# Smaller buffers for the modulation sums and the latents' weights, and the rotary tables on VectorE beside the second output gates

## The chip, the cores and the metric

The kernel runs on one core of one Trainium2 chip. The metric is the device time of one execution in microseconds (us), as a median over several executions. The engines that appear below are PE (TensorE: matrix products and transposes), DVE (VectorE), ACT (ScalarE), POOL (GpSimd) and SP (SyncE, which here only issues transfers between device memory and the core's on-chip buffers).

## The reference, cut to what matters

A trunk of two layers over 1,024 tokens of width 1,024, everything in f32. Layer 0 is an mLSTM mixer and an MLP, layer 1 is latent attention and an MLP, and between them a shared latent key and value is made. Every norm is modulated by sums over a vector `c`, and the rotary tables are a sine and a cosine of position times frequency.

```python
# layer 0: mLSTM mixer
proj = h @ w_in                                # q, k, v, input and forget gates, output gate og
lf = log_sigmoid(f_pre); b = cumsum(lf)        # per chunk of 128 tokens
hh = rmsnorm(mlstm_chunkwise(q, k, v, i_pre, f_pre), head_g)
out = (hh * sigmoid(og)) @ w_out
# every modulated norm: shift, scale and gate come from c
mod = silu(c) @ ada_w + ada_b                  # likewise kv_ada_w for the shared latent
h = rmsnorm(x, g) * (1 + scale) + shift
# shared latent key and value, rotary part
ckv, k_rope = split(h @ w_a); ang = positions[..., None] * inv
k_rope = apply_rope(k_rope, cos(ang), sin(ang))
```

## The kernel before

**Products.** The tokens are handled in two halves of 512 (`hfs[0]`, `hfs[1]`). Every f32 product is three fp32r matmuls (`mm3`, L280 to L282): high part times high part, high times low, low times high. A block of 128 outputs over the width of 1,024 is thus 24 matmuls. A weight block is loaded by SP into a `raw` buffer (128x1024), then `wsplit` copies its high part on ACT (L238, into `wh`) and subtracts on DVE to get the low part (L239, into `wl`).

**Buffers.** The rings that matter are `raw` (4 buffers of 128x1024), `ws` for split weights (8), `tmc` (6 of 128x512), `tma` (1 of 128x512), `hd` (8) and `k` (24, from `k4`), and the PSUM rings `ps`, `pc` and `pm` with 2 each. A buffer is reused when its last reader is done; a load into it waits on SP's in-order queue until then, and everything behind it in that queue waits too.

**Order.** Each engine executes its own instructions in program order. That order is set at build time by a scheduler with priorities (`prompt` raises one); `paced()` says that an instruction of the background may be issued only after a given one of the main work.

**Stages, in time.** The first gates are `gates_in(hfs[0])` and, in it, `gates0`: the 16 gate columns are transposed (L640), and a chain of small DVE and ACT instructions on 8 rows (L694 to L730) ends in transposes on PE (L743). Some POOL memsets clear or fill parts of its tiles (L615, L618, L625, L730). Behind it come values and intra-chunk work (`v_in`; `intra0`, whose exponentials are L769). Before all that, `drain(rope_tables())` has put the whole making of the rotary tables into the program: a position row is turned into angles and reduced by seven steps of a product and a sum of 128x1024 on POOL (L2535, L2536), then two `Sin` on ACT (L2541, L2542). The second output gates are `og0(hfs[1], k4v)`: eight blocks of projection, each followed by Exp, Ln and Exp on ACT (L682 to L684), while `split_o(hfs[1])` multiplies the heads by the gates (L797) and splits them into high (L800) and low part (L801) for the output projection, and `p0` does the first half's residual and norm.

**Background.** `ada_chunk` makes four-times-128 modulation sums: four loads of 128x2x512 of `ada_w` or `kv_ada_w` into `raw` (L377), eight DVE sums into `tma` (L384), then four transposes (L364), a reduction and an addition. `latent_weights` loads six weight blocks of the latent projections into `raw` (L1563), sums them on DVE against the shift (L1567, L1569), scales them on ACT (L1573), splits them with `wsplit` and writes them to device memory from POOL's queue. The steps of both are taken one by one beside the main work:

```python
drain(rope_tables())
drain(with_bg(gates_in(hfs[0]), bgs, 1))
...
for k, _ in enumerate(og0(hfs[1], k4v)):
    if k % 2:
        prompt(next)(so)
    next(bgs)
    if k < 7:
        next(p0)
...
two_streams(f0, behind(bg_latent(), 5))
```

`f0` is the first MLP's sweeps over both halves (about 560 to 880 us). One step of `second` there loads two `raw` buffers of `w1` (L1020) and the first sum (L1025), combines them on DVE (L1026 and on) and makes the weights `wv` by a copy on ACT (L1030) and a subtraction on DVE (L1031); the up projection loads one `raw` buffer per step (L260). What is left of the modulation sums, and `latent_weights`, run beside it.

Of the kernel before, what the change touches and what calls it, by code (L numbers as in the profile page):

```python
# [9 lines left out]
F32 = mybir.dt.float32  # L10
# [4 lines left out]
ALU = mybir.AluOpType  # L15
# [67 lines left out]
def kernel(  # L83
# [286 lines left out]
    late = [False]  # L370

    def ada_chunk(w, c0, bias, dst):

        acc = tma()
        for q in range(4):
            r = raw().rearrange("p (a b) -> p a b", b=512)
            nc.sync.dma_start(r, wcols(w, c0, 512, 2 * q, 2))  # L377
            for kk in range(2):
                k = 2 * q + kk
                with paced():  # L380
                    if k == 0:
                        nc.vector.tensor_scalar(acc, r[:, kk], cond[:, 0:1], None, ALU.mult)
                    else:
                        nc.vector.scalar_tensor_tensor(  # L384
                            acc, r[:, kk], cond[:, k : k + 1], acc, ALU.mult, ALU.add
                        )
            yield
        yield
        late[0] = True
        yield "wait"  # L390
        late[0] = False
        yield from ada_turn(acc, bias, dst)
# [215 lines left out]
    def gates_in(hf):  # L608
# [6 lines left out]
        nc.gpsimd.memset(v7[:, :, 128:VE], 1.0)  # L615
        for t in range(4):
            v = k4()[:, : 7 * VE].rearrange("p (h e) -> p h e", e=VE)
            nc.gpsimd.memset(v[:, :, 128:VE], 1.0)  # L618
            hf.v.append([v[:, h_] for h_ in range(7)] + [v7[:, t], v])
# [5 lines left out]
        nc.gpsimd.memset(g[:, :, :, 8:32], 0.0)  # L625
# [63 lines left out]
    def gates0(hf):  # L689
# [40 lines left out]
        nc.gpsimd.memset(RM.bitcast(F32), 0.0)  # L730
# [822 lines left out]
    def latent_weights():  # L1553
# [4 lines left out]
        for b, vs in enumerate(views):  # L1558
            A, sh = (Akv, kvada[:, 0:8]) if b < 3 else (Aq, adac(1, SH1))
            r_ = raw()  # L1560
            r = r_.rearrange("p (a b) -> p a b", b=P)
            for c0, v in vs:
                nc.sync.dma_start(r[:, :, c0 : c0 + v.shape[2]], v)  # L1563
            yield
            acc = tma()[:, :P]
            with paced():
                nc.vector.tensor_scalar(acc, r[:, 0], sh[:, 0:1], None, ALU.mult)  # L1567
                for k in range(1, KD):
                    nc.vector.scalar_tensor_tensor(  # L1569
                        acc, r[:, k], sh[:, k : k + 1], acc, ALU.mult, ALU.add  # L1570
                    )
            for k in range(KD):
                nc.scalar.activation(r[:, k], r[:, k], AF.Identity, scale=A[:, k : k + 1])  # L1573
            for i, t in enumerate(wsplit(r_, D)):
# [6 lines left out]
            for _ in range(3 if b == 0 else 2):  # L1581
                yield "wait"
# [933 lines left out]
    def rope_tables():  # L2516
# [7 lines left out]
        d, a, kf = hd(), hd(), hd()  # L2524
        pi = d.bitcast(I32)
        nc.gpsimd.tensor_copy(d[:, 0:1], adac(0, SH1)[:, 7:8])
        nc.gpsimd.dma_start(pi, positions.to_broadcast([P, S]))
        nc.gpsimd.tensor_copy(a, pi)
        nc.gpsimd.tensor_scalar(a, a, inv, None, ALU.mult)
        yield  # L2530
        nc.gpsimd.tensor_scalar(kf, a, 1.0 / (2.0 * PI), MAGIC, ALU.mult, ALU.add)
        nc.gpsimd.tensor_scalar_add(kf, kf, -MAGIC)
        for part in TWO_PI_PARTS:
            yield
            nc.gpsimd.tensor_scalar(d, kf, -part, None, ALU.mult)  # L2535
            nc.gpsimd.tensor_add(a, a, d)  # L2536
        yield
        nc.gpsimd.tensor_scalar(a, a, 3.1415925, -3.1415925, ALU.min, ALU.max)
# [6 lines left out]
        nc.gpsimd.tensor_scalar(d, d, sg, None, ALU.mult)  # L2545
# [42 lines left out]
    drain(rope_tables())  # L2588
# [105 lines left out]
    so = split_o(hfs[1])  # L2694
    for k, _ in enumerate(og0(hfs[1], k4v)):
        if k % 2:
            prompt(next)(so)
        next(bgs)
        if k < 7:
            next(p0)  # L2700
# [115 lines left out]
    for v in f0:  # L2816
        if v != "within" and next(p1, end) is end:
            break
    two_streams(f0, behind(bg_latent(), 5))
    rope_perm()  # L2820
# [95 lines left out]
```

## Time and profile before

| | us |
|---|---|
| median of 3 runs | 2339.2 |
| the three runs | 2341.8, 2339.2, 2337.68 |
| the profiled execution | 2336.3 |
| its span, first to last instruction | 2334.1 |

| engine | busy us | instructions |
|---|---|---|
| PE | 2283.2 | 12,042 |
| DVE | 1704.7 | 2,749 |
| ACT | 1126.0 | 1,911 |
| POOL | 146.3 | 231 |

In the views, each instruction has its line, its operation and its tiles as output<-input. A wait is written as the idle time of an engine before an instruction, with the engine and the line that released it; "SPq" is SP's queue, "PEld" PE's weight loads, which overlap its matmuls. Windows give each engine's busy time and instruction count in a stretch, then the granted share of the full TensorE clock, the busy share of the transfer engines and the rate in GB/s.

### The profile page before, as it was taken

What the parts mean: (1) busy time and instruction counts of PE and PEld (TensorE: products, weight loads), DVE (VectorE), ACT (ScalarE), POOL (GpSimd) and SP (SyncE); (2) the same over time, 40 slices, a digit from 0 to 9 for tenths busy, and PEclk for the clock granted to TensorE, in tenths of its full rate; (3) what the DMA queues carried; (4) which work ended last, traced back from release to release, by engine and by line L of the source; (5) the groups of instructions that cost most, each with busy time, mean ns of one, the idle gap of its engine ahead of it and who ended that gap; (6) DMA issues with size and microseconds to landing.
All of it is one profiled execution on the core that took longest, in us unless ns stands there. A gap on an engine that the chain in (4) does not pass through costs nothing.

```text
span 2334.1 us, 32606 instructions
## 1 busy us (share of the span) xinstructions
PE 2283.2 (98%) x12042; PEld 1922.5 (82%) x12042; DVE 1704.7 (73%) x2749; ACT 1126.0 (48%) x1911; POOL 146.3 (6%) x231
## 2 busy tenths in 40 slices
PE   8899999999999999999999999999999999999998
PEld 6788798888877778778888778888888888989997
DVE  6776776879778777678774687765666488798776
ACT  4275334665335355544454464444444444655543
POOL 2700000000112220000000000000000000000000
PEclk9999999999999999999999999999999999999999
DMA  9452464657899888566686754874434452455432
GB/s 328 142 166 82 146 198 139 197 185 230 292 291 296 276 292 301 173 216 213 215 266 188 239 181 149 262 249 136 145 100 136 118 167 81 147 156 166 133 109 109
DMA packets 401103, 444.37 MB, mean 190 GB/s; under 512 B 26579, under 2 KB 288784, under 8 KB 400944
## 3 DMA queue, kind: packets, MB, share of 16 engines
q1 hardware_dynamic: 388000, 397.09, 53.7%
q0 software_dynamic: 12944, 45.20, 5.4%
q8 instruction: 95, 1.56, 0.3%
q14 instruction: 64, 0.52, 0.1%
HBM read 343.65 MB, written 98.57 MB: 189 GB/s over the span
## 4 chain that ended last, share of the span: by engine, by line
PE 77%; DVE 9%; DMA 8%; ACT 2%; issue 2%; SPq 1%; DVEq 0%; ACTq 0%
PE ps L280 13%; PE ps L282 12%; PE ps L281 12%; PE pm L280 9%; PE pm L281 9%; PE pm L282 8%; DMA raw<-in_mlp_w_dram 5%; PE pc L281 2%; PE pc L282 2%; PE pc L280 2%; DVE wl L239 1%; DMA raw<-in_a_w_in_dram 1%; PE pc L1969 1%; DVE k L247 1%; PE pm L1774 1%
## 5 line engine op out<-in xcount | busy, mean ns | idle before, releaser
L239 DVE TENSOR_TENSOR wl<-raw,wh 128x1024 fp32r<-128x1024 f32 (+5 forms) x323 | 382.6, 1187 | 210.2 <-ACT wh L238 185.3
L238 ACT CAST wh<-raw 128x1024 fp32r<-128x1024 f32 (+5 forms) x323 | 327.3, 1017 | 421.0 <-PE ps L281 164.7
L280 PE MATMUL ps<-k,wh 128*128 128x512 f32 (+1 forms) x1252 | 475.7, 380 | 5.6 <-DVE tmp L247 2.8
L282 PE MATMUL ps<-k,wl 128*128 128x512 f32 (+1 forms) x1252 | 467.9, 374 | 0.3 <-DVE wl L239 0.3
L281 PE MATMUL ps<-k,wh 128*128 128x512 f32 (+1 forms) x1252 | 467.7, 374 | 0.1
L280 PEld LDWEIGHTS ps<-k,wh 128*128 128x128 f32 x1252 | 235.9, 188 | 51.6 <-DVE tmp L247 3.6
L282 PEld LDWEIGHTS ps<-k,wl 128*128 128x128 f32 x1252 | 235.8, 188 | 42.9 <-DVE wl L239 0.9
L281 PEld LDWEIGHTS ps<-k,wh 128*128 128x128 f32 x1252 | 236.0, 188 | 41.9 <-issue 1.4
L247 DVE TENSOR_TENSOR k<-k,pm 128x512 f32<-128x512 f32 (+1 forms) x250 | 192.4, 801 | 62.7 <-PE pm L282 62.1
L280 PE MATMUL pm<-wh,hd 128*128 128x512 f32 x488 | 193.4, 396 | 2.6 <-ACT raw L1780 1.5
L282 PE MATMUL pm<-wh,hd 128*128 128x512 f32 x488 | 190.4, 390 | 0.0
L281 PE MATMUL pm<-wl,hd 128*128 128x512 f32 x488 | 190.4, 390 | 0.0
L384 DVE SCALAR_TENSOR_TENSOR tma<-raw,cond,tma 128x512 f32<-128x512 f32 x168 | 126.9, 755 | 23.3 <-DMA raw<-in_ada_w_dram 14.2
L280 PEld LDWEIGHTS pm<-wh,hd 128*128 128x128 f32 x488 | 91.7, 188 | 24.1 <-ACT raw L1780 4.0
L282 PEld LDWEIGHTS pm<-wh,hd 128*128 128x128 f32 x488 | 91.6, 188 | 19.9 <-DVE hd L494 0.5
L281 PEld LDWEIGHTS pm<-wl,hd 128*128 128x128 f32 x488 | 91.8, 188 | 18.4 <-issue 0.5
L281 PE MATMUL pm<-hd,wk 128*128 128x512 f32 x256 | 100.0, 391 | 1.7 <-DVE hd L494 1.7
L280 PE MATMUL pm<-hd,wk 128*128 128x512 f32 x256 | 100.8, 394 | 0.6 <-ACT hd L493 0.6
L1780 ACT ACTIVATE raw<-pm,sm 128x128 f32<-128x128 f32 (+3 forms) x64 | 47.5, 743 | 110.8 <-DVE sm L1779 107.2
L280 PE MATMUL pm<-hd,wh 128*128 128x512 f32 x256 | 99.5, 390 | 0.9 <-DVE tma L384 0.9
L282 PE MATMUL pm<-hd,wl 128*128 128x512 f32 x256 | 99.7, 390 | 0.5 <-DVE wl L239 0.5
L282 PE MATMUL pm<-hd,wk 128*128 128x512 f32 x256 | 99.8, 390 | 0.0
(494 smaller groups left out, 4857.5 us busy)
## 6 DMA issues: line engine op xcount, KB each, us to landing
raw<-in_mlp_w_dram SPq DMA_DIRECT2D x176, 512.0 KB, 4.6
raw<-in_ada_w_dram SPq DMA_DIRECT2D x80, 512.0 KB, 4.8
raw<-in_mlp_w_dram SPq DMA_DIRECT2D x128, 256.0 KB, 4.6
raw<-in_a_w_in_dram SPq DMA_DIRECT2D x44, 512.0 KB, 4.5
lo<-wl POOLq DMA_DIRECT2D x32, 512.0 KB, 7.0
wk<-lo SPq DMA_DIRECT2D x64, 256.0 KB, 3.8
xs<-k SPq DMA_DIRECT2D x40, 256.0 KB, 4.4
raw<-in_a_w_out_dram SPq DMA_DIRECT2D x16, 512.0 KB, 4.5
```

The lines of the kernel that those rows point to most:

```text
L238: nc.scalar.copy(hi[:, :n], r[:, :n])
L239: i = nc.vector.tensor_sub(lo[:, :n], r[:, :n], hi[:, :n].bitcast(F32))
L247: return f(*a, **k)
L280: nc.tensor.matmul(o, lh, rh, start=start, stop=False)
L281: nc.tensor.matmul(o, lh, rl, start=False, stop=False)
L282: pe_last[0] = nc.tensor.matmul(o, ll, rh, start=False, stop=stop)
L384: nc.vector.scalar_tensor_tensor(acc, r[:, kk], cond[:, k : k + 1], acc, ALU.mult, ALU.add)
L1774: nc.tensor.matmul(o[:, :w], qh, kh, start=False, stop=True)
L1780: nc.scalar.activation(pr[:, :n], f, AF.Exp, bias=m, scale=SCALE, accum_out=l)
L1969: nc.tensor.transpose(pt[:, ts(2 * e + i, P)], u.prs[i][:, ts(b + e, P)], ident)
```

## The change

1. The memsets of the gates (L615, L618, L625, L730, of both halves) go from POOL to DVE.
2. `rope_tables` is no longer drained before the first gates. It is stepped twice after each block of the second half's output gates. Its arithmetic goes from POOL to DVE, and each pair of a product and a sum becomes one `scalar_tensor_tensor`. Its tiles come from `k4` in place of `hd`, and a copy that only made it wait is left out. The two `Sin` stay on ACT.
3. `ada_chunk`, while `f0` runs, loads two `tmc` tiles of 128x512 with one transfer each, where it loaded one `raw` buffer.
4. `latent_weights` loads two `tmc` tiles in place of one `raw` buffer, and its scaling and split come one step after its sums; the split is made of halves of 128x512.

```diff
@@ -367,22 +367,28 @@
         nc.vector.tensor_add(dst, s, bias)
         yield
 
-    late = [False]
+    late, apart = [False], [False]
 
     def ada_chunk(w, c0, bias, dst):
 
         acc = tma()
         for q in range(4):
-            r = raw().rearrange("p (a b) -> p a b", b=512)
-            nc.sync.dma_start(r, wcols(w, c0, 512, 2 * q, 2))
+            if apart[0]:
+                r = [tmc(), tmc()]
+                for kk in range(2):
+                    nc.sync.dma_start(r[kk], w[ts(2 * q + kk, P), c0 : c0 + 512])
+            else:
+                r = raw().rearrange("p (a b) -> p a b", b=512)
+                nc.sync.dma_start(r, wcols(w, c0, 512, 2 * q, 2))
+                r = [r[:, 0], r[:, 1]]
             for kk in range(2):
                 k = 2 * q + kk
                 with paced():
                     if k == 0:
-                        nc.vector.tensor_scalar(acc, r[:, kk], cond[:, 0:1], None, ALU.mult)
+                        nc.vector.tensor_scalar(acc, r[kk], cond[:, 0:1], None, ALU.mult)
                     else:
                         nc.vector.scalar_tensor_tensor(
-                            acc, r[:, kk], cond[:, k : k + 1], acc, ALU.mult, ALU.add
+                            acc, r[kk], cond[:, k : k + 1], acc, ALU.mult, ALU.add
                         )
             yield
         yield
@@ -612,17 +618,17 @@
 
         hf.v = []
         v7 = sb.tile([P, 4 * VE], F32, tag="v7", bufs=1, name=f"v7_{hf.i}").rearrange("p (t e) -> p t e", e=VE)
-        nc.gpsimd.memset(v7[:, :, 128:VE], 1.0)
+        nc.vector.memset(v7[:, :, 128:VE], 1.0)
         for t in range(4):
             v = k4()[:, : 7 * VE].rearrange("p (h e) -> p h e", e=VE)
-            nc.gpsimd.memset(v[:, :, 128:VE], 1.0)
+            nc.vector.memset(v[:, :, 128:VE], 1.0)
             hf.v.append([v[:, h_] for h_ in range(7)] + [v7[:, t], v])
         n = 272
         ws_ = [
             wload([(0, 0, wcols(w_in, 1792, n, k0, nk))], n) for k0, nk in ((0, 3), (3, 3), (6, 2))
         ]
         g = tmc()[:, :256].rearrange("p (t a b) -> p t a b", a=2, b=32)
-        nc.gpsimd.memset(g[:, :, :, 8:32], 0.0)
+        nc.vector.memset(g[:, :, :, 8:32], 0.0)
         for t in range(4):
             pt = ps()[:, :n]
             for k in range(KD):
@@ -727,7 +733,7 @@
         nc.vector.tensor_add(enm, b, M)
         nc.scalar.activation(enm, enm, AF.Exp, scale=-1.0)
         RM = hf.RM = tmc(F32R)
-        nc.gpsimd.memset(RM.bitcast(F32), 0.0)
+        nc.vector.memset(RM.bitcast(F32), 0.0)
         nc.vector.tensor_scalar(RM[0:8], M, -1.0, None, ALU.mult)
         nc.vector.scalar_tensor_tensor(
             RM[32:40], M, -1.0, RM[0:8].bitcast(F32), ALU.mult, ALU.subtract
@@ -1557,28 +1563,36 @@
         views += [[(0, wcols(b_w_q_a[0], m * P))] for m in range(3)]
         for b, vs in enumerate(views):
             A, sh = (Akv, kvada[:, 0:8]) if b < 3 else (Aq, adac(1, SH1))
-            r_ = raw()
-            r = r_.rearrange("p (a b) -> p a b", b=P)
+            r = [tmc(), tmc()]
+            cols_ = lambda t: t.rearrange("p (a b) -> p a b", b=P)
             for c0, v in vs:
-                nc.sync.dma_start(r[:, :, c0 : c0 + v.shape[2]], v)
+                for i in range(2):
+                    nc.sync.dma_start(cols_(r[i])[:, :, c0 : c0 + v.shape[2]], v[:, ts(i, 4)])
             yield
             acc = tma()[:, :P]
+            of = lambda k: r[k // 4][:, ts(k % 4, P)]
             with paced():
-                nc.vector.tensor_scalar(acc, r[:, 0], sh[:, 0:1], None, ALU.mult)
+                nc.vector.tensor_scalar(acc, of(0), sh[:, 0:1], None, ALU.mult)
                 for k in range(1, KD):
                     nc.vector.scalar_tensor_tensor(
-                        acc, r[:, k], sh[:, k : k + 1], acc, ALU.mult, ALU.add
+                        acc, of(k), sh[:, k : k + 1], acc, ALU.mult, ALU.add
                     )
+            yield "wait"
+            hi = sb.tile([P, 1024], F32R, tag="ws", bufs=WS, name=f"wh_{next(uid)}")
+            lo = sb.tile([P, 1024], F32R, tag="ws", bufs=WS, name=f"wl_{next(uid)}")
             for k in range(KD):
-                nc.scalar.activation(r[:, k], r[:, k], AF.Identity, scale=A[:, k : k + 1])
-            for i, t in enumerate(wsplit(r_, D)):
+                nc.scalar.activation(of(k), of(k), AF.Identity, scale=A[:, k : k + 1])
+            for i in range(2):
+                nc.scalar.copy(hi[:, ts(i, 512)], r[i])
+                nc.vector.tensor_sub(lo[:, ts(i, 512)], r[i], hi[:, ts(i, 512)].bitcast(F32))
+            for i, t in enumerate((hi, lo)):
                 if b == 2:
 
                     f = lambda t: t.rearrange("p (a b) -> p a b", b=P)[:, :, ts(i, 64)]
                     nc.gpsimd.dma_start(f(lw[b, 0]), f(t).bitcast(F32))
                 else:
                     nc.gpsimd.dma_start(lw[b, i], t.bitcast(F32))
-            for _ in range(3 if b == 0 else 2):
+            for _ in range(2 if b == 0 else 1):
                 yield "wait"
             pt = pc()
             nc.tensor.transpose(pt[:, :P], acc, ident)
@@ -2521,28 +2535,26 @@
         for q in range(4):
             nc.vector.memset(sg[ts(q, 32), :], 1.0 if q % 2 else -1.0)
         MAGIC = 1.5 * 2.0**23
-        d, a, kf = hd(), hd(), hd()
+        d, a, kf = k4()[:,:1024],k4()[:,:1024],k4()[:,:1024]
         pi = d.bitcast(I32)
-        nc.gpsimd.tensor_copy(d[:, 0:1], adac(0, SH1)[:, 7:8])
         nc.gpsimd.dma_start(pi, positions.to_broadcast([P, S]))
-        nc.gpsimd.tensor_copy(a, pi)
-        nc.gpsimd.tensor_scalar(a, a, inv, None, ALU.mult)
+        nc.vector.tensor_copy(a, pi)
+        nc.vector.tensor_scalar(a, a, inv, None, ALU.mult)
         yield
-        nc.gpsimd.tensor_scalar(kf, a, 1.0 / (2.0 * PI), MAGIC, ALU.mult, ALU.add)
-        nc.gpsimd.tensor_scalar_add(kf, kf, -MAGIC)
+        nc.vector.tensor_scalar(kf, a, 1.0 / (2.0 * PI), MAGIC, ALU.mult, ALU.add)
+        nc.vector.tensor_scalar_add(kf, kf, -MAGIC)
         for part in TWO_PI_PARTS:
             yield
-            nc.gpsimd.tensor_scalar(d, kf, -part, None, ALU.mult)
-            nc.gpsimd.tensor_add(a, a, d)
+            nc.vector.scalar_tensor_tensor(a, kf, -part, a, ALU.mult, ALU.add)
         yield
-        nc.gpsimd.tensor_scalar(a, a, 3.1415925, -3.1415925, ALU.min, ALU.max)
+        nc.vector.tensor_scalar(a, a, 3.1415925, -3.1415925, ALU.min, ALU.max)
         nc.vector.scalar_tensor_tensor(kf, a, -1.0, a, ALU.mult, ALU.max)
         nc.vector.tensor_scalar(kf, kf, -1.0, PI / 2, ALU.mult, ALU.add)
         nc.scalar.activation(d, a, AF.Sin)
         last = nc.scalar.activation(kf, kf, AF.Sin)
         with tc.issue_after(last.ins):
             nc.scalar.preload_act_table_set("natural_log_exp_and_others")
-        nc.gpsimd.tensor_scalar(d, d, sg, None, ALU.mult)
+        nc.vector.tensor_scalar(d, d, sg, None, ALU.mult)
         nc.gpsimd.dma_start(rope_d[1], d)
         nc.gpsimd.dma_start(rope_d[0], kf)
         yield
@@ -2585,7 +2597,6 @@
             nc.sync.dma_start(
                 xt_d[0][2 * b * P : (2 * b + 2) * P].rearrange("(k p) n -> p k n", p=P), xT0.t[b]
             )
-    drain(rope_tables())
     drain(with_bg(gates_in(hfs[0]), bgs, 1))
     drain(with_bg(qk_last(hfs[0]), bgs, 1))
     x1 = load_x1()
@@ -2692,10 +2703,13 @@
     ms = [Mlp(0, False)]
     p0 = post(hfs[0], y0, B0, x_ahead(k4v, True), A1, adac(0, SH2), ms[0], (2, 2, 2, 5, 1))
     so = split_o(hfs[1])
+    tables = rope_tables()
     for k, _ in enumerate(og0(hfs[1], k4v)):
         if k % 2:
             prompt(next)(so)
         next(bgs)
+        for _ in range(2):
+            next(tables, None)
         if k < 7:
             next(p0)
     y1 = FH(claim=True)
@@ -2816,7 +2830,9 @@
     for v in f0:
         if v != "within" and next(p1, end) is end:
             break
+    apart[0] = True
     two_streams(f0, behind(bg_latent(), 5))
+    apart[0] = False
     rope_perm()
```

In the order of the program these edits move instructions at three places. Names end in running numbers, which differ between the two kernels.

The first place is POOL at the first gates: `hd_610` to `hd_612` are the table tiles, `k_105` to `k_108` the value tiles. Before:

```order
L2532 TENSOR_SCALAR hd_612<-hd_612 128x1024
L2535 TENSOR_SCALAR hd_610<-hd_612 128x1024
L618 MEMSET k_105_644 128x7x2
L618 MEMSET k_106_646 128x7x2
L618 MEMSET k_107_648 128x7x2
L618 MEMSET k_108_650 128x7x2
L2536 TENSOR_TENSOR hd_611<-hd_611,hd_610 128x1024
L2535 TENSOR_SCALAR hd_610<-hd_612 128x1024
```

Now:

```order
L2533 DMA inv<-in_inv_freq_dram 32x1
L2540 DMA k_656_3940<-in_positions_dram 128x1024
L2558 DMA rope_d<-k_656_3940 128x1024
L2559 DMA rope_d<-k_658_3942 128x1024
L173 MEMSET k_728_4349 128x1
```

POOL has only the transfers of the tables left, and no arithmetic and no memset between the start and the first MLP.

The second place is DVE and ACT at the second output gates, DVE first: `hd_2568` is a head tile that L803 (before: L797) gates, `k_656` to `k_658` are the table tiles. Before:

```order
L797 SCALAR_TENSOR_TENSOR hd_2610<-hd_2610,cols,k_649_3929 128x512
L239 TENSOR_TENSOR wl_4204<-raw_4201,wh_4203 128x1024
L797 SCALAR_TENSOR_TENSOR hd_2610<-hd_2610,cols,k_649_3929 128x512
L801 TENSOR_TENSOR k_668_4015<-hd_2610,k_667_4014 128x1024
L486 TENSOR_SCALAR tmc_4094<-pc_4092 128x512
```

Now:

```order
L803 SCALAR_TENSOR_TENSOR hd_2568<-hd_2568,cols,k_646_3887 128x512
L2541 CAST k_657_3941<-k_656_3940 128x1024
L2542 TENSOR_SCALAR k_657_3941<-k_657_3941,inv 128x1024
L2544 TENSOR_SCALAR k_658_3942<-k_657_3941 128x1024
L2545 TENSOR_SCALAR k_658_3942<-k_658_3942 128x1024
L239 TENSOR_TENSOR wl_4196<-raw_4193,wh_4195 128x1024
L2548 SCALAR_TENSOR_TENSOR k_657_3941<-k_658_3942,k_657_3941 128x1024
L803 SCALAR_TENSOR_TENSOR hd_2568<-hd_2568,cols,k_646_3887 128x512
L2548 SCALAR_TENSOR_TENSOR k_657_3941<-k_658_3942,k_657_3941 128x1024
L807 TENSOR_TENSOR k_668_3991<-hd_2568,k_667_3990 128x1024
```

The table's instructions now stand between the two gatings and the split of one head tile. On ACT, at the last blocks of the same stage, before:

```order
L682 ACTIVATE k_652_3932<-ps_4268 128x512
L683 ACTIVATE k_652_3932<-k_652_3932 128x512
L238 CAST wh_4499<-raw_4497 128x1024
L682 ACTIVATE k_652_3932<-pm_4320 128x512
L684 ACTIVATE k_652_3932<-k_652_3932 128x512
L683 ACTIVATE k_652_3932<-k_652_3932 128x512
L684 ACTIVATE k_652_3932<-k_652_3932 128x512
L800 CAST k_673_4020<-hd_3119 128x1024
```

Now:

```order
L688 ACT_TABLE_LOAD
L688 ACTIVATE k_649_3890<-ps_4260 128x512
L688 ACTIVATE k_649_3890<-pm_4312 128x512
L689 ACT_TABLE_LOAD
L689 ACTIVATE k_649_3890<-k_649_3890 128x512 x2
L690 ACT_TABLE_LOAD
L690 ACTIVATE k_649_3890<-k_649_3890 128x512 x2
L482 ACTIVATE tmc_4248<-hd_3290 128x512
L2554 ACT_TABLE_LOAD
L2554 ACTIVATE k_658_3942<-k_658_3942 128x1024
L2556 ACT_TABLE_LOAD
L806 CAST k_673_3996<-hd_3077 128x1024
```

Five loads of a function table and the second `Sin` (L2554) now stand between the third split of the heads and the last one (L806); the first `Sin` (L2553) with its own load stands ahead of them.

The third place is SP in the first MLP's sweeps, where a step of `second` loads two buffers of `in_mlp_w` and one of `m`. Before:

```order
L1025 DMA k_1066_6224<-m_3924 128x512
L377 DMA raw_6274<-in_ada_w_dram 128x2x512
L377 DMA raw_6278<-in_ada_w_dram 128x2x512
L377 DMA raw_6282<-in_ada_w_dram 128x2x512
L377 DMA raw_6286<-in_ada_w_dram 128x2x512
L1025 DMA k_1089_6329<-m_3924 128x512
L1020 DMA raw_6325<-in_mlp_w_dram 128x8x128
L1020 DMA raw_6326<-in_mlp_w_dram 128x8x128
```

Now:

```order
L1031 DMA k_1081_6217<-m_3882 128x512
L1026 DMA raw_6213<-in_mlp_w_dram 128x8x128
L379 DMA tmc_6318<-in_ada_w_dram 128x512
L379 DMA tmc_6319<-in_ada_w_dram 128x512
L379 DMA tmc_6324<-in_ada_w_dram 128x512
L1026 DMA raw_6214<-in_mlp_w_dram 128x8x128
L379 DMA tmc_6325<-in_ada_w_dram 128x512
L1026 DMA raw_6258<-in_mlp_w_dram 128x8x128
L1031 DMA k_1089_6262<-m_3882 128x512
L1026 DMA raw_6259<-in_mlp_w_dram 128x8x128
L1026 DMA raw_6371<-in_mlp_w_dram 128x8x128
L1026 DMA raw_6372<-in_mlp_w_dram 128x8x128
```

The background's loads no longer take `raw` buffers, and several loads of MLP weights stand in a row behind them. Over the whole of `f0` the background issues 27 loads by L377 and 7 by L1563 before; 54 by L379 and 14 by L1570 now.

## The prediction

> **What bounds the kernel now.** I read the totals first, then PE's waits by stage, then windows and timelines where PE waits.
>
> ```profile
> span 2334.1 us, 32606 instructions
> PE 2283.2 (98%) x12042; PEld 1922.5 (82%) x12042; DVE 1704.7 (73%) x2749; ACT 1126.0 (48%) x1911; POOL 146.3 (6%) x231
> ```
>
> PE is busy 98% of the span, and the change adds and removes no matmul. So only two things can be gained: PE's idle time, 50.9 us in all, and stretches in which the granted clock is low because PE has stood still. What can be lost is any cover that DVE or ACT has now. I therefore ask of each of the three stages that the change touches what PE waits for there.
>
> At the first gates (76 to 150 us), the waits of PE and the windows around them:
>
> ```profile
> PE pc L743 <- DVE tmc L712: 6.1, 1, 6.1
> PE pc L762 <- ACT tmc L769: 1.0, 1, 1.0
> PE pc L743 <- ACT tmc L726: 0.9, 1, 0.9
> 92.00:98.20 6.20, 0.10 (x2) 0.01 (x1) 6.06 (x8) 0.00 (x0) 6.03 (x3) 0.70 0.00 0
> 98.20:101.30 3.10, 3.10 (x15) 3.08 (x16) 3.00 (x4) 0.00 (x0) 3.02 (x2) 0.50 0.00 0
> 107.60:111.60 4.00, 3.77 (x18) 3.45 (x18) 3.89 (x10) 0.00 (x0) 0.00 (x0) 0.57 0.34 92
> ```
>
> PE stands still for 6.1 us until DVE's L712 is done, while DVE and POOL are both busy throughout, and the granted clock (the number behind the POOL column) is 0.50 for the 3.1 us after it. No transfer moves in these 9.3 us (the last two columns), so no load is what is missing.
>
> **Part 1, the first gates.** Why DVE is late is seen by holding its rows against those of the same code for the second half of the tokens, where POOL does nothing:
>
> ```profile
> 82.68 2.60 DVE L696 TENSOR_SCALAR tmc<-tmc,cols 8x512 f32<-8x512 f32 x1
> ...
> 88.22 2.76 DVE L704 SCALAR_TENSOR_TENSOR tmc<-tmc,tmc 8x512 f32<-8x512 f32 x1
> 90.91 1.51 DVE L705 SCALAR_TENSOR_TENSOR tmc<-tmc,tmc 8x512 f32<-8x512 f32 x1
> ...
> 93.17 4.26 DVE L709 TENSOR_TENSOR_SCAN tmc<-ones,tmc 8x128 f32<-8x128 f32 x4
> 97.46 0.68 DVE L712 TENSOR_TENSOR tmc<-tmc,tmc 8x512 f32<-8x512 f32 x1
> ...
> 241.88 0.47 DVE L696 TENSOR_SCALAR tmc<-tmc,cols 8x512 f32<-8x512 f32 x1
> ...
> 244.76 0.68 DVE L704 SCALAR_TENSOR_TENSOR tmc<-tmc,tmc 8x512 f32<-8x512 f32 x1
> 247.82 0.67 DVE L705 SCALAR_TENSOR_TENSOR tmc<-tmc,tmc 8x512 f32<-8x512 f32 x1
> ...
> 252.43 1.35 DVE L709 TENSOR_TENSOR_SCAN tmc<-ones,tmc 8x128 f32<-8x128 f32 x4
> ```
>
> These four lines take 11.13 us in the first half and 3.17 in the second: 2.13 + 2.08 + 0.84 + 2.91 = 8.0 us of excess on the chain to L712. What runs beside them is POOL's table arithmetic, of which this is the first instruction of each of the seven steps; the step's sum follows it (the row behind it is a memset that the change moves to DVE):
>
> ```profile
> L2535 POOL TENSOR_SCALAR hd<-hd x7: 2770/2782/3631, 61.5 to 96.1; 128x1024 f32<-128x1024 f32 x7
> 84.47 0.53 POOL L730 MEMSET tmc<- 128x512 f32 x1
> ```
>
> With the tables gone from here I expect 8.0 us less on the chain, and the memset of L730 is 0.53 more on DVE if it stands ahead of L712: some 7.4. L712 is then done at 98.14 − 7.4 = 90.7, and PE gets to L743 at 92.1 (98.2 less the wait of 6.1), so 1.4 us of slack are left and the 6.1 us go. With the stop goes the slow clock behind it: half of 3.10 is 1.55 us. The stretch at 107.6 has a clock of 0.57 for 3.77 us of work, which is another 0.43 × 3.77 = 1.62; it stands behind the 0.9 us wait on L726, at the end of the same chain, whose part after L712 was also slowed. Sum 6.1 + 1.55 + 1.62 + 0.9 = 10.2 us, and up to 1.0 more from L769. On ACT stand four loads of function tables there, of which these are the first and the last, 1.28 us each, and two `Sin`:
>
> ```profile
> 121.59 1.28 ACT L2541 ACT_TABLE_LOAD   x1
> 122.89 1.06 ACT L2541 ACTIVATE hd<-hd 128x1024 f32<-128x1024 f32 x1
> ...
> 130.83 1.28 ACT L2544 ACT_TABLE_LOAD   x1
> ```
>
> They are 4 × 1.28 + 2 × 1.06 = 7.2 us, and they leave ACT in the middle of L769's exponentials, for which PE waits. All of it gone would be 11.2. I take −10: of the late small waits some will come back, because PE arrives earlier and the other work of ACT and DVE does not shrink. The ends are −11.2 and −6 (the stop goes, and a later wait eats the clock's part).
>
> **Part 2, the second output gates.** Here the tables' work arrives. Prices from the one table instruction of each kind that DVE already had, and from the stage as it stands:
>
> ```profile
> L2539 DVE SCALAR_TENSOR_TENSOR hd<-hd x1: 1214/1214/1214, 122.9 to 122.9; 128x1024 f32<-128x1024 f32 x1
> L2540 DVE TENSOR_SCALAR hd<-hd x1: 678/678/678, 125.4 to 125.4; 128x1024 f32<-128x1024 f32 x1
> 380.00:415.00 35.00, 35.00 (x167) 28.69 (x164) 22.03 (x41) 20.65 (x37) 0.10 (x1) 1.00 0.57 178
> 415.00:443.00 28.00, 28.00 (x127) 23.20 (x126) 27.96 (x40) 20.33 (x31) 0.69 (x7) 1.00 0.68 211
> 443.00:450.00 7.00, 7.00 (x31) 5.45 (x30) 1.23 (x2) 0.49 (x1) 0.00 (x0) 1.00 0.47 149
> 450.00:500.00 50.00, 50.00 (x220) 41.01 (x219) 37.65 (x51) 31.56 (x48) 1.63 (x3) 1.00 0.48 153
> 442.44 1.06 ACT L800 CAST k<-hd 128x1024 fp32r<-128x1024 f32 x1 [1.16 <-DVE hd L797]
> ```
>
> DVE gets seven steps and L2539's kind (8 × 1.21), six instructions of L2540's kind (6 × 0.68) and a conversion of 128x1024 that no row shows: between these two rows' 0.68 and 1.21, 0.9 taken. That is 9.7 + 4.1 + 0.9 = 14.7 us. ACT gets two `Sin` and six table loads, since Exp and Ln each load again between the two: 2 × 1.06 + 6 × 1.28 = 9.8 us. Nothing can be won here, as PE does not wait at all. What covers it: DVE is idle for 13.0 us in 380 to 415, almost never in 415 to 443, 5.8 in 443 to 450 and 12.4 in 450 to 500. The last gating (L797), the copy (L800) and the subtraction (L801) end the stage, and behind them the output projection waits for the split head.
>
> Is there room? In the order of the changed kernel, the last split's copy (L806) stands behind the last gate's Exp, three table loads, Ln and Exp, a square, the second `Sin` and its loads: from the last gate block's end on PE 0.59 + 2 × 1.28 + 4 × 0.63 + 0.63 + 1.28 + 1.06 + 1.28 + 1.06 = 11.0 us, with 0.63 for a Ln, Exp or square of 128x512 (an estimate from L2541's 1.06 for twice the length). ACT may be late when the chain begins by the first `Sin` and two loads, 3.6 us: 14.6 in all. In PE's order of the changed kernel, 73 matmuls stand between that block's end and the first use of the last split tile (51 before), and at 50.00 us for 220 matmuls that is 16.6 us. So about 2 us are left, and I take +1 for a stop that the windows can't exclude; the ends are 0 and +6.5 (DVE's 14.7 us find only the 5.8 idle ones of 443 to 450 and run 8.9 late, less the 2 of slack and rounded down). The transfers that come along (one of positions, two of the tables, on POOL's queue) meet a transfer share of 0.5 to 0.7: nothing.
>
> **Part 3, the first MLP.** PE's waits in 600 to 860, what SP's queue waits for in 560 to 900, and windows:
>
> ```profile
> PE ps L282 <- DVE wv L1031: 3.8, 4, 1.3
> PE ps L280 <- ACT wv L1030: 3.6, 2, 2.1
> SPq L1020 <- DVE wl L239: 46.0, 14, 9.3
> SPq L1020 <- DVE wv L1031: 33.1, 12, 6.1
> SPq L377 <- DVE wl L239: 17.6, 12, 2.4
> 600.00:860.00 260.00, 247.28 (x1076) 198.94 (x1075) 201.59 (x293) 104.89 (x167) 54.35 (x77) 0.99 0.89 289
> 860.00:900.00 40.00, 40.00 (x179) 33.06 (x178) 30.60 (x38) 19.44 (x28) 5.81 (x13) 1.00 0.90 332
> ```
>
> PE is idle for 260.00 − 247.28 = 12.7 us, and a granted clock of 0.99 is some 2 us of 247 (the figure is rounded): about 15 us are to be had at most. PE waits for `wv`, so for weights that come late, and SP waits with the weight loads (L1020) for the subtractions that free a `raw` buffer. A step needs two of the four buffers, the up projection one, and the background takes the last. Is it the buffers or the rate of transfers? At 860 to 900 the same traffic runs at 332 GB/s and PE stands still for nothing; 600 to 860 needs
>
> ```profile
> DMA packets 68389, 75.06 MB, mean 289 GB/s; under 512 B 4818, under 2 KB 54529, under 8 KB 68373
> ```
>
> 75.06 MB in 247 us of PE's work, 303 GB/s, below those 332. So I put the waits down to the ring, which the change relieves of 34 loads, and take −8, half of it rounded up. The ends are −15, and +15 if the queue turns against it (below).
>
> **Part 4, the small things.** The background splits its loads: 34 more issues on SP at
>
> ```profile
> L377 SPq DMA_DIRECT2D raw<-in_ada_w_dram x16: 367/368/442, 603.2 to 676.0; - x16
> ```
>
> 0.37 us each, 12.6 us on a queue that waits for buffers in the rows above for 97 us. Latents' splits become 12 copies and 12 subtractions of half the length where 6 of each were; they cost some 0.2 us more per pair beside the 58.4 us that DVE is idle in 600 to 860. The memsets that DVE takes over are the 0.53 of L730 and shorter ones. I take 0 for all of it; if DVE had no idle time it would be 2 us.
>
> **The sum.** −10 + 1 − 8 = −17 on the profiled 2336.3: 2319.3. The median of the runs shown, 2339.2, stands 2.9 above the profiled execution, so 2322.
>
> **Rivals.** A difference under 0.2% (4.7 us: 2334.5 to 2343.9) can't be told from no change.
>
> First, *transfers bound the first MLP anyway*. For it: a transfer share of 0.89 in the window. Against it: 860 to 900. Then part 3 gives nothing: 2339.2 − 9 = 2330. Chance 0.20.
>
> Second, *the second output gates give a stop back*. For it: DVE has 0.04 us idle of 28 there, and the room that I worked out is 2 us of 16. At the upper end +6.5 in place of +1: 2322 + 5.5 = 2327. Chance 0.12. The rows of part 1 show a load at 121.59 and its `Sin` at 122.89, so 1.30 us from the one to the other and nothing more. By the Trainium skill, "ScalarE: Activation LUTs", section "What ACT_TABLE_LOAD costs", each switch of tables costs a drain of about 1.38 us beside the load; five switches on the chain would by that page be an estimated 6.9 us more, the room would be gone, and this rival would come true. The trace speaks against the drain.
>
> Third, *the stop at the first gates stays*, bound by something other than POOL, and the other parts give little: about 2337. For it: the slack of 1.4 us that I work out for L743 is small, and the 0.9 us wait on ACT's L726 shows a second late releaser. Chance 0.08.
>
> Fourth, on the other side, *SP's queue turns against the change*. SP issues in order. The background's loads now wait for `tmc` tiles, which come free only when a paced DVE sum has read them, and all six tiles serve it; MLP weights stand in the queue behind such a load. Before, a background load waited for a buffer that the main work's own splits freed (L377 <- L239). If this holds weights back once per step, PE's idle time in this stage doubles, slow clock included: +15 in place of −8, so 2322 + 23 = 2345. It decides once the extra waits exceed the 9 us won elsewhere plus the 4.7. For it: SP's queue waits 46.0 us in 14 waits for one kind of buffer already, up to 9.3 at once. Against it: the sums are short, and DVE is idle for 58.4 of 260 us. Chance 0.10.
>
> **How the numbers follow.** Forecast 0.50, with a range of its own of 2314 (part 3 at its upper gain) to 2331 (part 1 at −6, part 3 halved); the rivals 0.20, 0.12, 0.08 and 0.10. The time is the forecast's, 2322. The range 2312 to 2338 takes in the first three rivals and leaves out the fourth and the forecast's lower tail, some 2 in 10. Faster: 0.50, most of the first rival (0.17) and of the second (0.09), 0.76. Same: the rest of these and the third, 0.14. Slower: the fourth, 0.10.
>
> **What would show it.** At the first gates, L696 and L704 of the first half should take some 0.5 and 0.7 us, the 6.1 us wait on L712 be gone and the granted clock stay at 1.00 until 110 us; if they stay long, POOL was not the cause. At the second output gates, PE should show no wait on L806 or L807 above 1 us. In the first MLP, PE's idle time should fall from 12.7 to about 5 us, and SP's waits with L1026 (before: L1020) on L239 should shrink. If they turn into waits for `tmc` sums (L390), the fourth rival is at work. The prediction is wrong if the first MLP's PE idle time does not fall, or if PE stops between 430 and 460 us.

## The result and the profile after

| | median us | runs |
|---|---|---|
| before | 2340.47 | 4 (2337.68 to 2341.8) |
| changed | 2323.66 | 4 (2321.05 to 2324.77) |

The ratio is 0.9928, 95% interval [0.9911, 0.9945]: 16.8 us less, where 17 were forecast. The profiled execution of the changed kernel took 2324.77 us. The totals of its page:

```profile
span 2323.0 us, 32695 instructions
PE 2282.0 (98%) x12042; PEld 1924.9 (83%) x12042; DVE 1702.7 (73%) x2782; ACT 1130.3 (49%) x1919; POOL 92.5 (4%) x196
```

PE's busy time differs by only 1.2 us, so most of the gain is PE's idle time: 50.9 us before, 41.0 now. The two profiled executions lie 11.5 us apart (2336.3 and 2324.77), less than the medians do, so the stages below add up to the smaller figure. At the first gates, the whole list of PE's waits between 60 and 150 us is one row; windows of the same stretches as before follow (engines' busy time, granted clock, transfer share, GB/s):

```profile
PE pc L791 <- ACT tmc L775: 0.5, 1, 0.5
```

```profile
92.00:98.20 6.20, 6.20 (x52) 5.99 (x51) 5.93 (x16) 1.93 (x4) 0.00 (x0) 1.00 0.25 97
98.20:101.30 3.10, 3.10 (x32) 2.66 (x31) 3.02 (x7) 0.37 (x1) 0.00 (x0) 1.00 0.38 95
107.60:111.60 4.00, 4.00 (x38) 3.37 (x36) 3.41 (x6) 2.22 (x8) 0.00 (x0) 1.00 0.78 257
```

PE no longer stands still and the clock stays at 1.00. DVE's timeline shows why (lines are six later than before: L718 was L712):

```profile
83.96 0.47 DVE L702 TENSOR_SCALAR tmc<-tmc,cols 8x512 f32<-8x512 f32 x1
...
86.30 0.68 DVE L710 SCALAR_TENSOR_TENSOR tmc<-tmc,tmc 8x512 f32<-8x512 f32 x1
...
88.81 1.36 DVE L715 TENSOR_TENSOR_SCAN tmc<-ones,tmc 8x128 f32<-8x128 f32 x4
90.20 0.68 DVE L718 TENSOR_TENSOR tmc<-tmc,tmc 8x512 f32<-8x512 f32 x1
```

The instructions that took 2.60, 2.76 and 4.26 us take 0.47, 0.68 and 1.36. L718 ends at 90.88, and PE reaches its transposes (L749) at 93.80: 2.9 us of slack.

At the second output gates, windows 10 us earlier than those of before, and ACT's timeline at the end of the stage:

```profile
370.00:405.00 35.00, 35.00 (x175) 28.71 (x174) 26.92 (x46) 20.86 (x39) 0.00 (x0) 1.00 0.53 160
405.00:433.00 28.00, 28.00 (x127) 23.19 (x126) 28.00 (x38) 19.39 (x27) 0.07 (x1) 1.00 0.54 174
433.00:440.00 7.00, 7.00 (x32) 5.82 (x31) 5.87 (x9) 6.93 (x10) 0.48 (x1) 1.00 0.92 274
440.00:490.00 50.00, 50.00 (x218) 40.67 (x217) 39.99 (x53) 36.65 (x53) 2.56 (x12) 1.00 0.58 184
```

```profile
434.08 0.59 ACT L688 ACTIVATE k<-pm 128x512 f32<-128x512 f32 x1
434.69 1.28 ACT L689 ACT_TABLE_LOAD   x1
...
440.14 1.28 ACT L2554 ACT_TABLE_LOAD   x1
441.44 1.06 ACT L2554 ACTIVATE k<-k 128x1024 f32<-128x1024 f32 x1
442.51 1.28 ACT L2556 ACT_TABLE_LOAD   x1
443.81 1.05 ACT L806 CAST k<-hd 128x1024 fp32r<-128x1024 f32 x1
```

PE is busy in every one of the 120 us although DVE has nothing to spare in 405 to 433. In the first MLP, windows, PE's waits and SP's waits (550 to 890 us):

```profile
590.00:850.00 260.00, 256.44 (x1134) 211.11 (x1133) 209.69 (x309) 111.50 (x181) 59.00 (x81) 0.99 0.90 295
850.00:890.00 40.00, 37.17 (x162) 29.87 (x162) 28.15 (x35) 18.08 (x26) 2.93 (x9) 1.00 0.85 304
```

```profile
PE ps L280 <- DVE tmp L247: 3.6, 2, 1.9
PE pm L280 <- ACT hd L499: 1.8, 1, 1.8
```

```profile
SPq L1026 <- DVE wv L1037: 41.1, 13, 6.8
...
SPq L1026 <- DVE wl L239: 34.8, 13, 7.9
...
SPq L379 <- DVE tma L390: 22.8, 30, 2.2
```

PE's idle time fell from 12.7 to 3.6 us, then comes 2.8 in 850 to 890, where it was none. The waits for `wv` are gone. SP's two waits with MLP loads, though, hardly fell: 46.0 + 33.1 before, 34.8 + 41.1 now.

### The profile page after: what moved, and what is told of

The parts are those of the page before. It is cut to its first block, busy times and chain, and to the rows that moved or that the text cites. A ratio compares the mean times of both kernels' runs of the same rounds, so it can differ in the third digit from the quotient of the medians.

```text
span 2323.0 us, 32695 instructions
## 1 busy us (share of the span) xinstructions
PE 2282.0 (98%) x12042; PEld 1924.9 (83%) x12042; DVE 1702.7 (73%) x2782; ACT 1130.3 (49%) x1919; POOL 92.5 (4%) x196
## 4 chain that ended last, share of the span: by engine, by line
PE 82%; DVE 7%; DMA 6%; issue 2%; ACT 2%; SPq 1%; POOL 0%; DVEq 0%; ACTq 0%; POOLq 0%
PE ps L280 14%; PE ps L282 14%; PE ps L281 14%; PE pm L280 9%; PE pm L281 9%; PE pm L282 9%; PE pc L281 2%; PE pc L280 2%; PE pc L282 2%; DMA raw<-in_mlp_w_dram 2%; DMA raw<-s 1%; DVE wl L239 1%; PE pc L1983 1%; DVE k L247 1%; PE pm L1788 1%
## 5 line engine op out<-in xcount | busy, mean ns | idle before, releaser
L238 ACT CAST wh<-raw 128x1024 fp32r<-128x1024 f32 (+2 forms) x317 | 321.3, 1016 | 453.9 <-PE ps L281 178.6
L239 DVE TENSOR_TENSOR wl<-raw,wh 128x1024 fp32r<-128x1024 f32 (+2 forms) x317 | 372.5, 1176 | 209.8 <-ACT wh L238 180.9
L390 DVE SCALAR_TENSOR_TENSOR tma<-raw,cond,tma 128x512 f32<-128x512 f32 x120 | 89.5, 746 | 16.0 <-DMA raw<-in_kv_ada_w_dram 8.3
L280 PE MATMUL pm<-hd,wh 128*128 128x512 f32 x256 | 99.3, 390 | 1.8 <-ACT hd L499 1.8
L281 PE MATMUL pm<-hd,wh 128*128 128x512 f32 x256 | 99.7, 390 | 0.2 <-DVE hd L500 0.2
```

The costliest lines, as they stand in the source:

```text
L238: nc.scalar.copy(hi[:, :n], r[:, :n])
L239: i = nc.vector.tensor_sub(lo[:, :n], r[:, :n], hi[:, :n].bitcast(F32))
L280: nc.tensor.matmul(o, lh, rh, start=start, stop=False)
L281: nc.tensor.matmul(o, lh, rl, start=False, stop=False)
L390: nc.vector.scalar_tensor_tensor(acc, r[kk], cond[:, k : k + 1], acc, ALU.mult, ALU.add)
```

## The experiments

Each was timed beside the kernel before on the same chip, and chips differ, so ratios count. "PE waits" is the sum of the rows of PE's waits in 560 to 900 us, from one profile each; "ACT late" is ACT's wait in that stretch for MLP weights at the high part's copy (L238), from the same profiles (a dash: under 1 us).

| kernel | median us | ratio [95%] | PE waits | ACT late |
|---|---|---|---|---|
| before | 2340.47 | 1 | 12.6 | 23.8 |
| changed | 2323.66 | 0.9928 [0.9911, 0.9945] | 6.4 | - |
| changed, again | 2322.28 | 0.9923 [0.9910, 0.9937] | 6.9 | - |
| tables and memsets only | 2331.95 | 0.9966 [0.9953, 0.9978] | 9.7 | 21.1 |
| tables only | 2325.65 | 0.9949 [0.9937, 0.9962] | 11.4 | 26.6 |
| small buffers only | 2329.26 | 0.9955 [0.9941, 0.9969] | 6.4 | - |
| changed, latents as before | 2325.04 | 0.9941 [0.9924, 0.9958] | 6.9 | 3.9 |
| changed, sums as before | 2330.15 | 0.9965 [0.9953, 0.9977] | 11.9 | 20.5 |
| before, split transfers | 2332.72 | 0.9980 [0.9971, 0.9990] | 7.2 | 20.2 |

### The two halves of the change

```diff
-    apart[0] = True          # and latent_weights as before
```

> The changed kernel without its small buffers: modulation sums and latents' weights load into raw buffers as before. If the three places add up as forecast (first gates -10, second output gates +1, first MLP -8), this keeps the first two: about 2331 us against 2340.5 before, no wait on the first gates' L712, and PE idle in the first MLP for about 12 us as before. If transfers bound the first MLP anyway and all was won at the first gates, it stays at the changed kernel's 2324. If the tables' work at the second output gates costs nothing, 2330.

The ratio of 0.9966 is 8.0 us less than 2340.47; the forecast had 9 for these two places. L718's wait is gone, and PE waits in the MLP much as before (9.7 us against 12.6). The complement is the kernel before with only `ada_chunk`'s and `latent_weights`' new loads:

> The kernel before with the small buffers alone (modulation sums and latents' weights in tmc tiles during the first MLP); tables and memsets stay on POOL ahead of the first gates. If the three places add up: 2340.5 - 8 = 2332, the 6.1 us wait on L712 unchanged, PE idle in the first MLP for about 5 us. If transfers bound the first MLP: 2340. If the queue of SP turned against the change and only the first gates paid: over 2341.

0.9955, or 10.5 us less; forecast 8. The two ratios multiply to 0.9921, and the whole change has 0.9928 and 0.9923: the parts add up, and the rival that transfers bound the MLP falls. The wait at the first gates stayed but was 3.7 us here, not 6.1.

### What the small buffers do

```diff
-            r = [tmc(), tmc()]     # latent_weights: one raw, scaled and split at once
+            r_ = raw()
```

> The changed kernel with latent_weights as before (one raw buffer each, scaling and split in the same step); the modulation sums keep their small buffers. If it is the raw ring that holds the first MLP, in proportion to loads that leave it (27 of 34): 2324 + 2 = 2326. If the latents' part carries the gain, because their scaling and split hold a raw buffer longest: 2324 + 5 = 2329 or more.

```diff
-    apart[0] = True                # the sums stay in raw
```

> The changed kernel, but the modulation sums load into raw as before also in the first MLP; only the latents keep small buffers and the later scaling and split. By the number of loads that leave the ring (7 of 34): 2332 less 1 to 2, so about 2330. If the latents carry half of the gain, 2327.

With the sums' buffers alone the ratio is 0.9941, with the latents' alone 0.9965; without either it is 0.9966. So the sums carry most of the gain, though even 0.9941 and 0.9966 have intervals that just touch. The latents alone gain nothing, and what they add to the sums, 3 to 4 us (0.9941 against 0.9928 and 0.9923), these runs don't resolve. The second kernel's waits, from one profile, are instructive:

```profile
PE ps L280 <- DVE tmp L247: 4.7, 5, 1.7
PE ps L280 <- ACT tmp L980: 1.4, 1, 1.4
PE ps L280 <- DVE k L247: 1.1, 1, 1.1
PE ps L282 <- DVE wv L1037: 1.0, 1, 1.0
```

The waits for `wv` fell to 1.0 us, and the time came back as waits for sums of products.

Is it the ring or the size of the transfers? One kernel splits the transfers and keeps the `raw` buffer:

```diff
-            nc.sync.dma_start(r, wcols(w, c0, 512, 2 * q, 2))
+            for kk in range(2):    # in the first MLP only
+                nc.sync.dma_start(r[:, kk], w[ts(2 * q + kk, P), c0 : c0 + 512])
```

> The kernel before, with the modulation sums' loads of the first MLP split into two transfers of 128x512 each, but still into one raw buffer. If it is the raw buffers that hold the first MLP, nothing changes: 2340 with PE idle there for some 12 us. If smaller transfers alone make weights come earlier, 2333 or less.

0.9980, between the two expectations: 4.7 us of gain, interval 2.3 to 6.8. In the kernel before, DVE waits in this stretch for the sums' transfers, and here it nearly stops to:

```profile
DVE tma L384 <- DMA raw<-in_ada_w_dram: 5.4, 6, 1.4
```

```profile
DVE tma L388 <- DMA raw<-in_ada_w_dram: 0.8, 2, 0.5
```

DVE executes in order, so a sum that waits for a late 512 KB holds up the weights' subtractions behind it; with two of 256 KB the first sum starts earlier. That the 4.7 us come this way is read from these waits and not shown by a run. What splitting does not give is early weights: "ACT late" stays at 20.2. In this table it falls only where the sums leave the ring. In the kernel before, and in the changed one with latents as before:

```profile
ACT wh L238 <- DMA raw<-in_mlp_w_dram: 23.8, 18, 4.5
```

```profile
ACT wh L238 <- DMA raw<-in_mlp_w_dram: 3.9, 3, 2.7
```

Then a fifth `raw` buffer, paid for with a `tmc` and a `tmp` buffer, beside a control that only pays:

```diff
-RAW = 4
+RAW = 5                            # not in the control
-TMP = 3
-TMC = 6
+TMP = 2
+TMC = 5
```

> The kernel before with five raw buffers instead of four, paid for with one tmc and one tmp buffer less. If the raw ring is what holds the first MLP, PE's waits for wv there shrink to a third or less and this is 6 to 10 us faster than the control with four raw buffers. If the ring is not the cause (but the size of the transfers, or their rate), within 3 us of the control.

> The control: the kernel before with four raw buffers, and one tmc and one tmp buffer less. Waits for wv in the first MLP as before (about 7 us together); the smaller rings may cost something elsewhere, so 2338 to 2350.

2366.01 us, ratio 1.0114 [1.0100, 1.0128], and 2373.83, 1.0141 [1.0127, 1.0155]. The medians are 7.8 us apart, as the ring theory said, but its other sign failed. In 560 to 900 us PE's waits for `wv` are 3.2 us with five buffers and 4.6 with four, far from a third. "ACT late" is 32.4 us with five and 15.0 with four, and in 620 to 870 PE idles 11.1 us with five and 7.4 with four. Where the 7.8 us were won the profiles can't say, because the two profiled executions took 2370.61 and 2368.26 us, the other way round. With five buffers PE's longest waits in the MLP were for the background itself:

```profile
PE pc L364 <- DVE tma L384: 6.5, 3, 4.2
```

So one more buffer is not the same as moving the background out of the ring, and the pair does not show that a full ring is what PE waited for in the MLP. With smaller `tmc` and `tmp` rings in both, it does not say either how much of the gain the ring alone would give.

### POOL against DVE

Taking work off POOL, and moving it away, are two things. First the tables on DVE at their old place, ahead of the first gates:

```diff
+    drain(rope_tables())
     drain(with_bg(gates_in(hfs[0]), bgs, 1))
...
-            next(tables, None)
```

> The changed kernel, but the tables are drained at their old place ahead of the first gates, on DVE. This separates taking the work off POOL from moving it away. If POOL was what stretched DVE's instructions, the 8-row instructions stay short here too (L710 0.68 us, L715 1.36 for four), but five table instructions and a wait for the first Sin stand inside the chain, some 7 us less 2.9 of slack: PE waits about 4 us for L718, and the time is 2328 to 2332. If the place and not POOL was the cause, the wait is 6 us or more and the time 2333 or above.

2331.05 us, ratio 0.9969 [0.9957, 0.9982]. By the ratio that is 2333 on the scale of 2340.47, at the border of the two expected cases, so the durations decide and not the time. DVE's timeline of it:

```profile
89.86 0.68 DVE L710 SCALAR_TENSOR_TENSOR tmc<-tmc,tmc 8x512 f32<-8x512 f32 x1
...
93.72 0.68 DVE L711 SCALAR_TENSOR_TENSOR tmc<-tmc,tmc 8x512 f32<-8x512 f32 x1 [2.64 <-ACT tmc L709]
...
95.15 1.36 DVE L715 TENSOR_TENSOR_SCAN tmc<-ones,tmc 8x128 f32<-8x128 f32 x4
```

At the same place and with more work on DVE, the 8-row instructions are short: POOL's arithmetic stretched them. The chain is late now through the tables in it and ACT's table loads. PE idles 4.9 us in 60 to 150 at a clock of 0.94, but in five waits further on, none of them for L718, so the place of the stop was forecast wrongly. Taking the arithmetic off POOL without moving it gains no time that shows: with the small buffers alone, tables and memsets still on POOL, the ratio is 0.9955.

The counterpart keeps the arithmetic on POOL, at the new place:

```diff
-        nc.vector.scalar_tensor_tensor(a, kf, -part, a, ALU.mult, ALU.add)
+        nc.gpsimd.tensor_scalar(d, kf, -part, None, ALU.mult)
+        nc.gpsimd.tensor_add(a, a, d)
```

> The changed kernel, but the tables' arithmetic stays on POOL (product and sum apart, as before) at its new place beside the second output gates. If POOL's work is what slowed DVE at the first gates, some 45 us of it now slow DVE in a stage in which it has no idle time: DVE's L807 and L239 there take over 1.5 us instead of 1.22, PE stops at the output projection for 3 to 12 us, and the time is 2327 to 2336. If only the short 8-row instructions suffer, or if DVE's load and not POOL's was what mattered: the changed kernel's 2324 or less, since DVE has 14.7 us less to do.

2331.73, ratio 0.9964 [0.9951, 0.9977]: some 8 us slower than the changed kernel, though DVE has less to do. POOL took up the tables' arithmetic at 356 us, while the last chunks were still under way. From the timelines of DVE, POOL and PE, and a window:

```profile
362.63 0.16 DVE L859 SCALAR_TENSOR_TENSOR sm<-sm 128x4 f32<-128x4 f32 x1
...
367.54 2.13 DVE L859 SCALAR_TENSOR_TENSOR sm<-sm 128x4 f32<-128x4 f32 x1
...
441.39 3.41 DVE L807 TENSOR_TENSOR k<-hd,k 128x1024 fp32r<-128x1024 f32 x1
```

```profile
367.28 2.37 POOL L2549 TENSOR_TENSOR k<-k,k 128x1024 f32<-128x1024 f32 x1
```

```profile
372.72 1.09 PE L890 MATMUL pc<-ident,tmc 128*128 128x128 f32 x4 [4.00 <-DVE tmc L864]
```

```profile
370.00:400.00 30.00, 27.28 (x131) 22.77 (x132) 25.50 (x39) 15.96 (x34) 21.17 (x8) 0.89 0.27 74
```

L807 takes 3.41 us here, where it takes 1.21 in the changed kernel; L239 mostly keeps its 1.22. The stop is at the end of the chunks (L864), not at the output projection: 2.7 us idle and 0.11 of 27.3, 3.0 us, by the clock in this window. L859, a few steps ahead of L864 in the same chain, took 2.13 us beside POOL's sum (L2549), and 0.16 five us earlier.

### The memsets

```diff
-        nc.vector.memset(RM.bitcast(F32), 0.0)
+        nc.gpsimd.memset(RM.bitcast(F32), 0.0)    # and the other three lines
```

> Only the tables are moved to DVE beside the second output gates: memsets on POOL, background loads in raw buffers as before. If the memsets are worth nothing, as forecast, the same as with the memsets: 2332. If a small POOL memset beside the gates' chain stretches a DVE instruction, up to 2334, with a wait on L718 or L732 in the first gates.

0.9949 against 0.9966 with the memsets on DVE; the intervals overlap. The window 150 to 370 us, with memsets on DVE and then on POOL:

```profile
150.00:370.00 220.00, 217.47 (x1405) 184.50 (x1403) 151.92 (x336) 94.34 (x202) 0.56 (x1) 1.00 0.45 134
```

```profile
150.00:370.00 220.00, 219.59 (x1422) 186.29 (x1421) 153.01 (x333) 94.90 (x203) 1.83 (x8) 1.00 0.45 135
```

2.5 us of idle time against 0.4. The same edit on the whole change, run beside the changed kernel itself:

> The changed kernel with its memsets back on POOL; tables on DVE at the new place and all small buffers stay. Without the small buffers the same edit went from 2332 to a ratio that is 0.0017 lower, and PE's idle time in 60 to 370 us from 3.1 to 0.4 us. If that is real, this runs 2 to 3 us faster than the changed kernel on the same chip, and PE no longer waits for a late weight split at 270 us. If it was scatter, the two are equal within 1.5 us.

> The changed kernel itself, on the chip of the runs beside it: ratio to the kernel before 0.993 as measured, 2321 to 2325.

2319.38 (ratio 0.9917 [0.9903, 0.9930]) beside 2322.28. Idle time in 150 to 370 is 0.5 against 2.6 us in their profiles. The medians differ by 2.9 us, as expected, while the intervals overlap: the idle time shows that the memsets on DVE cost some 2 us, and the times alone would not. That idle time is 1.7 to 3.3 us in each of the seven profiles here with memsets on DVE, and 0.3 to 0.5 in the five with memsets on POOL and rings of the old size.

## Why the prediction was right

**The sum.** −17 forecast, −16.8 measured. Tables with memsets gave −8.0 (forecast −10 + 1 + 0), small buffers −10.5 (forecast −8). That the total is right to 0.2 us is luck: by their ratios the tables alone gave −11.9 where −9 was forecast, the memsets took back 2 to 4 where 0 was, and the small buffers gave 2.5 more. The forecast's own range is also 1 us too wide at each end: from its terms it is 2315 to 2330.

**First gates, −10.** Right, with its mechanism: tables and memsets together gave 8.0. The long instructions shrank to the second half's durations, L718 was forecast to end at 90.7 and ended at 90.88, and the slow clock went with the stop. That agreement is partly luck: the chain began 1.29 us later (L694 at 79.83 before, L700 at 81.12 now), and the sum left out two more stretched instructions, L700 and L702, which took 1.40 and 0.78 us before and take 0.68 and 0.41 now (as L706 and L708). The second half's gates transposes, the last of L640 and now of L646, start at 236.6 before and at 226.9 after, 9.7 us earlier. That it is POOL's arithmetic is shown from both sides, by the tables on DVE at the old place and on POOL at the new one. The size is less sure than one trace suggests: the same code waited 6.1 us before, and 3.7 in the profiles of the small buffers alone and of the split transfers.

**Second output gates, +1.** PE lost nothing there: 0. The room held. The last gate block ended on PE at 430.45, its Exp began 3.6 us later, and L806 ended at 444.86: 14.4 us, where the sum had 14.6 to set against 16.6. The drain that the Trainium skill ("ScalarE: Activation LUTs", "What ACT_TABLE_LOAD costs") adds to each switch does not show: from a load's start to the next instruction's it is 1.30 us in the rows above, and PE did not stop. The second rival falls.

**The small things, 0.** This is the term that was mis-sized: memsets on DVE come with some 2 us of idle time in 150 to 370. I priced the memset's duration and not the order: with it PE's order changes, and at 270 us a weight's copy came 1.1 us late. The longer SP queue cost nothing that shows; its 30 waits for `tmc` are short (2.2 us at most).

**First MLP, −8.** The direction was right, the size 2.5 too small, and the reason given is at most part of it. The step that failed is "So I put the waits down to the ring". The ring's own share is not shown: "ACT late" is 20 to 27 us in each kernel of the table whose sums use `raw`, and 0 to 4 where they don't, but a fifth buffer made it longer. Two other things were in those waits. The size of the transfer is worth 4.7 us without relieving the ring, beside 5.9 for moving the sums to `tmc` (0.9966 to 0.9941), both with wide intervals. The other stood in the trace of before, and the prediction passed over it: the longest wait for `wv`, 2.13 us, ended at 820.53. ACT's and DVE's timelines ahead of it:

```profile
815.88 0.40 ACT L1573 ACTIVATE raw<-raw,mods 128x128 f32<-128x128 f32 x1 [0.46 <-DVE tma L1569]
817.18 1.18 ACT L1573 ACTIVATE raw<-raw,mods 128x128 f32<-128x128 f32 x3 [0.90 <-DVE tma L1569]
818.39 1.04 ACT L238 CAST wh<-raw 128x1024 fp32r<-128x1024 f32 x1
819.35 0.63 ACT L974 ACTIVATE tmp<-tmp 128x512 f32<-128x512 f32 x1
819.88 0.60 ACT L1030 CAST wv<-raw 128x512 fp32r<-128x512 f32 x1
```

```profile
814.90 0.69 DVE L1028 TENSOR_TENSOR raw<-k,raw 128x512 f32<-128x512 f32 x1
```

The weights for L1030 were ready at 815.59, and ACT got to them at 819.88, because the latents' scaling (L1573), which overwrites what the sums (L1569) still read, stood ahead of them in ACT's order and waited for each sum, with their copy (L238) behind it. That wait was ACT's order and not the ring: behind the same instructions it is 2.36 us where the sums have left the ring and 2.20 with split transfers. With the latents' later step alone, PE has no wait for ACT's `wv` left. Taken alone, though, that step moved the waits and not the time.

**The rivals.** Transfers bound the MLP anyway: no. SP's queue turns against the change: no. Its sign, waits for `tmc` sums (L390), did appear (22.8 us in 30 waits), but they were short, and PE's idle time fell. A small give-back came that no case had: 2.8 us idle in 850 to 890, 1.8 of them for a copy on ACT (L499). In 850 to 900, PE idles 1.7 to 2.8 us in every kernel with the latents' new step that ran here, and at most 0.1 in those with the old one and rings of the old size (0.6 and 1.6 in the two with smaller `tmc` and `tmp` rings).

## What to carry to other kernels

When one engine's instructions take two to six times what the same code takes elsewhere in the trace, look at what runs beside them before making the chain shorter; moving that neighbour's work to another engine and another place pays its stretch and the slow clock behind the stop. Here either move alone paid nothing that the runs resolve. A wait named for a late weight can come from a shared ring, a large transfer or another engine's order; the waits of the engines that make the weight (ACT and DVE here) suggest which, and a run with only that cause removed has to confirm it. Price an instruction that changes engines by the order that it brings, not by its duration alone.

## What was not expected of the hardware

POOL's effect on DVE goes by which POOL instruction runs beside it. The 8x512 instruction L696 took 2.60 us before, and 0.47 as L702 in the profile of the small buffers alone, with the same code at this place. Before, L696 began at 82.68, beside POOL's sum:

```profile
82.14 2.40 POOL L2536 TENSOR_TENSOR hd<-hd,hd 128x1024 f32<-128x1024 f32 x1
```

With the small buffers alone, L702 ran beside POOL's product:

```profile
84.89 0.47 DVE L702 TENSOR_SCALAR tmc<-tmc,cols 8x512 f32<-8x512 f32 x1
```

```profile
83.50 3.28 POOL L2549 TENSOR_SCALAR hd<-hd 128x1024 f32<-128x1024 f32 x1
```

In these two kernels and the one with POOL at the new place, a single DVE instruction that ran beside a sum was up to 2.2 us longer than elsewhere, and beside a product alone less than 1 us. How the two engines' instructions fall together differs between kernels with the same code here, and so does the stop. And ACT, which makes six loads of function tables between 421 and 444 us, needs 1.28 us for each, and the next instruction starts 1.29 to 1.30 us after the load's start.
